# Seven products for twelve instead of eight K tiles in the gate and value projections of an mLSTM layer

## The chip, the cores and the metric

The kernel runs on one core of a Trainium2 chip. The core has TensorE (PE) for matmuls, VectorE (DVE) and ScalarE (ACT) for elementwise work, GpSimd (POOL), SyncE (SP), which here only issues loads, and 16 DMA engines. The metric is device time in microseconds (us): the median of several executions. Lower is better.

## The reference

A trunk of two layers works on x of 256 tokens by 2048 channels, in float32. Each layer has a mixer and a gated feed-forward part. The second layer's mixer is an mLSTM with 8 heads of width 256; its input projection is the part that changes:

```python
def mlstm_mixer(h, w_in, b_gate, h_norm, w_out):
    proj = h @ w_in                       # 256 x 2048 times 2048 x (4*2048 + 32)
    q = heads(proj[..., :MLSTM_W]) * (MLSTM_HEAD_DIM ** -0.5)
    k = heads(proj[..., MLSTM_W:2 * MLSTM_W])
    v = heads(proj[..., 2 * MLSTM_W:3 * MLSTM_W])
    o_gate = jax.nn.sigmoid(proj[..., 3 * MLSTM_W:4 * MLSTM_W])
    gates = proj[..., 4 * MLSTM_W:] + b_gate
    ...                                   # forward and backward scans over the tokens, summed
    hn = rms_norm_per_head(hsum) * h_norm
    return (hn * o_gate) @ w_out
```

## The kernel before

**Matmuls.** Every float32 matrix is split into a high part (rounded by a cast on ACT) and a low part (the rest, by a subtraction on DVE), and a product is the sum of three matmuls: high by high, high by low, low by high. For weights this happens as they arrive. `Stream` (L95) runs through one long list of chunks of 128 x 1024 elements (512 KiB): `load` brings a chunk into one of 7 buffers w through SP's queue, `split` (L125) makes hl of it, in one of 4 buffers, by the cast of L136 and the subtraction of L137. `next` (L158) hands out the next chunk; it keeps loads 6 chunks and splits 2 chunks ahead of PE's place in the program. A chunk of the kind `Made` is loaded from a scratch in DRAM that the kernel has filled before. A chunk of the kind `Chain` gets two additions of half chunks on DVE before its split (L132, L133): the sum left by the chunk before is added to its first half, and its first half to its second.

**Order of the work.** PE's instructions run in the order of the program. The other engines' instructions are put in order by the scheduler of the framework, which simulates the program and takes what is ready, so work of DVE may run well before its place in the program. Small tasks (one head's scores, drains of PSUM, transposes) are generators in a `Weave` (L165): each product advances a clock by `tick`, and a task goes on when its time has come, so a number after `yield` sets where its next matmuls stand among the others. PSUM has two buffers "mm" of two banks and four "ps" of one bank.

**The mLSTM layer** (`mlstm_layer`, L775) runs over four pairs of heads, hp = 0 to 3. For each it makes queries and keys of two heads (tiles mq and mk, `stat_group`, 64 matmuls each, 16 chunks of weights in all) and starts the two tasks `head` (L863), which load a row of gates G, build masks from it (arg), multiply queries and keys (qk), scale (A), transpose (atr) and multiply with the values (av). Then, for hp = 0 to 2, `gates_values` (L989) makes the output gates of this pair (mo) and the values of the next pair (mv), 512 columns each, together. Call this stage the gate/value stage, and the one before it the query/key stage.

**Seven products.** Take two K tiles (128 rows of weights each) as a pair, the two halves of the tokens, and the two blocks of columns (gate, value). Done directly this is 8 products. In the way of Strassen it is 7, with sums of weights and sums of inputs. Three sums of weights come from s0, s1 and r: first m0 = s0 + s1, then r's first half + m0's, then r's second half + r's first. `premix` (L471) makes them ahead of time in DRAM, with DMAs that copy and accumulate: ten DMAs per pair, on the queues of ACT and POOL, each paced by the last matmul issued (L486). The sums of inputs are made by `combine` (L951) from the high and low parts and stand in the tile mcomb.

Before, ML_PAIRS = 4: K tiles 0 to 7 are four such pairs, tiles 8 to 15 are direct. A group runs in this order: direct tiles 8 to 11 into mo; for the four pairs the products p4, p6, p5 and one into mo (8 chunks, all made by premix); direct tiles 12 to 15 into mo; for the four pairs p0 and one into mo; then mv: four products of input sums, and the direct tiles 8 to 15. Two tasks drain PSUM: `first` (L1010) takes p4, p5 and p6 out, `second` (L1029) takes mo and p0 and then starts `gated` (L924), which makes the sigmoid with reciprocals on DVE (L933).

Premix for this layer is started inside the first layer's feed-forward part (L1293) with a gap of 30 us of the Weave's clock: one pair starts every 30 us, and its steps take 5 x 30 us. The feed-forward layers use seven products too, with units A and B (tiles pp); there every second pair is a `Chain` already.

Of the kernel before, what the change touches and what calls it, by code (L numbers as in the profile page):

```python
# [9 lines left out]
F32 = mybir.dt.float32  # L10
# [36 lines left out]
ML_PAIRS = 4  # L47
ML_DIRECT = (list(range(2 * ML_PAIRS, 12)), list(range(12, KT)))

# [45 lines left out]
class Stream:  # L95
# [29 lines left out]
    def split(self, then=None):  # L125
        i = self.n_split
        w, n, width = self.w.pop(i)
        if isinstance(self.srcs[i], Sum):
            self.sum = w
        elif isinstance(self.srcs[i], Chain):  # L130
            half = CH * P // 2
            self.behind(self.nc.vector.tensor_add(w[:, :half], w[:, :half], self.sum[:, :half]), self.lows[0])  # L132
            self.nc.vector.tensor_add(w[:, half:], w[:, half:], w[:, :half])  # L133
# [85 lines left out]
def trunk(ctx: ExitStack, tc: tile.TileContext, gx, xT, xn, call, catt, cml, weights, mixes, out):  # L219
# [257 lines left out]
    def premix(layer, gap, late, n):  # L477

        def one(i, s0, s1, r, made):
            m = scratch.tile([P, 2, CH * P], F32, tag=f"m{layer}{i}", name=f"m{layer}_{i}")  # L480
            h = CH * P // 2
            steps = [(nc.scalar, m[:, 0], s0, {}), (nc.scalar, m[:, 1], r, {}), (g, m[:, 0], s1, add),
                     (g, m[:, 1, :h], m[:, 0, :h], add), (g, m[:, 1, h:], m[:, 1, :h], add)]
            for n, (eng, to, src, kw) in enumerate(steps):
                for p in range(0, P, P // 2):
                    paced(eng.dma_start(to[p : p + P // 2], src[p : p + P // 2], **kw))  # L486
                    yield (0.1, 0.6, 0.6, 0.6, 0.6)[n] * gap
            for j in range(2):
                made[j].ap = m[:, j]
# [285 lines left out]
    def mlstm_layer(norm, nxt):  # L775
        with ExitStack() as es:
# [6 lines left out]
            comb = actp.tile([P, ML_PAIRS, 2, 4, P], F32R, tag="B1", name="mcomb")  # L783
# [79 lines left out]
            def head(h, q, kk, vt, hh):  # L863
# [6 lines left out]
                yield 2.5  # L870
# [80 lines left out]
            def combine(j):  # L951
# [9 lines left out]
                a.copy(comb[:, j, 0], sf)  # L961
                v.tensor_sub(comb[:, j, 1], sf, comb[:, j, 0].bitcast(F32))
# [18 lines left out]
            def direct(ps, kts, first, last):  # L981
                for i, k in enumerate(kts):
                    if i % 2 == 0:
                        hl = st.next()
                    wh, wl = (hl[:, j, i % 2 * 512 : i % 2 * 512 + 512] for j in range(2))
                    for t in range(2):
                        product(ps[:, t], x_part(k, t), wh, wl, first[t] and i == 0, last[t] and i == len(kts) - 1)

            def gates_values(hp):  # L989
# [5 lines left out]
                js = range(ML_PAIRS)  # L995

                mo = mmp.tile([P, 2, 512], F32, tag="mm", name=f"mo{hp}")
                direct(mo, ML_DIRECT[0], (True, True), (False, False))

                p46 = mmp.tile([P, 2, 512], F32, tag="mm", name=f"mp46{hp}")  # L1000
                p5 = psp.tile([P, 512], F32, tag="ps", name=f"mp5{hp}")
                for j in js:
                    xs = [[comb[:, j, i, m] for i in range(2)] for m in (1, 0, 2)] + [x_part(2 * j + 1, 1)]
                    for n, (ps, x_) in enumerate(zip((p46[:, 0], p46[:, 1], p5, mo[:, 1]), xs)):
                        if n % 2 == 0:
                            hl = st.next()
                        wh, wl = (hl[:, i, n % 2 * 512 : n % 2 * 512 + 512] for i in range(2))
                        product(ps, x_, wh, wl, n < 3 and j == 0, n < 3 and j == js[-1])

                def first():  # L1010
                    t5 = t1p.tile([P, 512], F32, tag="t5", name=f"mt5{hp}")
                    a.copy(t5, p5)
                    yield 1.2
                    for to, op, one, two in ((x10, v.tensor_sub, p46[:, 1], t5), (x01, v.tensor_sub, t5, p46[:, 0]),
                                             (x11, v.tensor_sub, x01, p46[:, 1])):
                        tc.keep_in_program_order(op(to, one, two))
                        yield 1.0

                wv.add(first(), 0.3)
                direct(mo, ML_DIRECT[1], (False, False), (False, True))  # L1020

                p0 = psp.tile([P, 512], F32, tag="ps", name=f"mp0{hp}")
                for j in js:
                    hl = st.next()
# [584 lines left out]
```

## Time and profile before

| | |
|---|---|
| median of 3 runs | 2148.92 us (2148.67 to 2149.26) |
| profiled execution | 2149.43 us, span 2147.6 us |
| PE busy | 2140.5 us |
| DVE, ACT, POOL busy | 1802.4, 1445.1, 306.3 us |
| DMA | 612.95 MB, mean 285 GB/s |
| gate/value stages (three) | 1043.07 to 1087.29, 1136.12 to 1180.34, 1229.17 to 1273.40 us |

The profile shows one execution. A row of a timeline gives start, duration, engine, line, operation, the tile written <- the tiles read, the shape and how many such records were merged; brackets hold idle time of the engine before it and what ended that. Rows of groups give busy us and mean ns of one, and after the second bar the idle time before. A row of waits gives total us, times, longest. Line numbers are those of kernel.py; matmuls have one line (L274), so they are told apart by their tiles. PEld is the load of the stationary operand, which runs beside the matmuls.

### The profile page before, as it was taken

How to read it: one execution, taken by the hardware profiler on the slowest of the kernel's cores; microseconds unless marked ns; L12 is line 12 of the kernel's file. 1: busy time of each engine (PE TensorE's matmuls, PEld its weight loads, DVE VectorE, ACT ScalarE, POOL GpSimd, SP SyncE). 2: the span in 40 equal slices, each digit the busy share in tenths (PEclk: the TensorE clock that was granted, in tenths of full speed). 3: DMA queues.
4: the chain of work that ended last, by engine and by line, in shares of the span. 5: the costliest groups of instructions: out<-in, count | busy, mean ns of one | idle time of the engine just before them, and what ended most of it. 6: DMA issues, size and time to landing. Idle time of an engine off the chain costs nothing.

```text
span 2147.6 us, 32448 instructions
## 1 busy us (share of the span) xinstructions
PE 2140.5 (100%) x11364; PEld 1834.2 (85%) x11364; DVE 1802.4 (84%) x2536; ACT 1445.1 (67%) x2199; POOL 306.3 (14%) x390
## 2 busy tenths in 40 slices
PE   9999999999999999999999999999999999999999
PEld 7888888888888888889888888888888888888887
DVE  7786678889988889898888797667888898889988
ACT  6665577777777777766556564557776777777774
POOL 0022112111111122111111011211111111100000
PEclk9999999999999999999999999999999999999999
DMA  9678889899999999998988798988999999888775
GB/s 333 209 213 257 260 250 321 270 326 337 312 331 329 339 350 339 312 301 240 289 244 296 234 310 237 279 244 248 312 288 335 335 314 317 286 256 270 254 250 187
DMA packets 184422, 612.95 MB, mean 285 GB/s; under 512 B 24282, under 2 KB 27138, under 8 KB 184258
## 3 DMA queue, kind: packets, MB, share of 16 engines
q1 hardware_dynamic: 133952, 478.60, 61.9%
q0 software_dynamic: 30304, 73.69, 20.1%
q10 hardware_dynamic: 20002, 58.60, 7.9%
q8 instruction: 89, 1.46, 0.3%
q14 instruction: 75, 0.61, 0.1%
HBM read 608.64 MB, written 111.19 MB: 335 GB/s over the span
## 4 chain that ended last, share of the span: by engine, by line
PE 94%; DVE 2%; DMA 2%; issue 1%; ACT 0%; ACTq 0%; DVEq 0%; SPq 0%
PE up L274 43%; PE pp L274 15%; PE op L274 8%; PE mk L274 4%; PE mq L274 4%; PE mo L274 3%; PE qproj L274 3%; PE dn L274 3%; PE mv L274 3%; PE mp L274 2%; DVE hl L137 1%; PE kproj L274 1%; PE vproj L274 1%; PE pool L274 1%; DMA w<-in_up 1%
## 5 line engine op out<-in xcount | busy, mean ns | idle before, releaser
L137 DVE TENSOR_TENSOR hl<-w,hl 128x1024 fp32r<-128x1024 f32 (+1 forms) x869 | 1045.7, 1214 | 167.4 <-ACT hl L136 158.0
L136 ACT CAST hl<-w 128x1024 fp32r<-128x1024 f32 (+1 forms) x868 | 892.0, 1046 | 391.6 <-PE up L274 112.5
L274 PE MATMUL up<-xx,hl 128*128 128x512 f32 (+1 forms) x5632 | 994.0, 337 | 0.0
L274 PEld LDWEIGHTS up<-xx,hl 128*128 128x128 f32 x5632 | 866.9, 188 | 130.6 <-DVE hl L137 0.7
L486 POOL DMA_DIRECT2D m<-m x208 | 166.4, 816 | 931.2 <-PE up L274 431.8
L274 PE MATMUL pp<-hl,s 128*128 128x512 f32 x912 | 227.2, 390 | 1.3 <-DVE hl L137 1.0
L274 PEld LDWEIGHTS pp<-hl,s 128*128 128x128 f32 x912 | 167.9, 188 | 36.3 <-DVE hl L137 3.7
L274 PE MATMUL pp<-hl,g 128*128 128x512 f32 x684 | 174.0, 390 | 0.0
L274 PEld LDWEIGHTS pp<-hl,g 128*128 128x128 f32 x684 | 125.9, 188 | 24.5
L440 ACT COPY tb_up<-up 128x512 f32<-128x512 f32 x88 | 51.6, 587 | 112.6 <-PE up L274 112.6
L1122 DVE TENSOR_TENSOR y<-y,z 128x510 f32<-128x510 f32 x88 | 60.7, 690 | 62.9 <-ACT y L1121 62.4
L486 POOL DMA_DIRECT2D m<-in_dn x80 | 69.0, 863 | 245.8 <-PE up L274 57.9
L1121 ACT ACTIVATE y<-tb_up,conv 128x256 f32<-128x256 f32 x176 | 103.7, 589 | 0.0
L274 PE MATMUL mk<-xx,hl 128*128 128x512 f32 (+1 forms) x512 | 93.3, 338 | 1.2 <-DVE hl L137 1.2
L274 PE MATMUL mq<-xx,hl 128*128 128x512 f32 (+1 forms) x512 | 92.2, 337 | 0.0
L274 PE MATMUL op<-hl,cat 128*128 128x512 f32 x384 | 91.5, 393 | 0.0
L1119 ACT ACTIVATE z<-tb_up,conv 128x256 f32<-128x256 f32 x176 | 88.4, 502 | 4.0 <-DVE tb_up L1114 2.0
L274 PEld LDWEIGHTS mk<-xx,hl 128*128 128x128 f32 x512 | 79.2, 188 | 12.9 <-DVE hl L137 1.6
L274 PE MATMUL op<-hl,mcat 128*128 128x512 f32 x384 | 89.7, 392 | 0.0
L441 DVE TENSOR_TENSOR tb_up<-up,tb_up 128x512 f32<-128x512 f32 x88 | 60.7, 690 | 34.1 <-ACT tb_up L440 33.7
L274 PEld LDWEIGHTS mq<-xx,hl 128*128 128x128 f32 x512 | 79.3, 188 | 11.6
L1120 ACT ACTIVATE z<-tb_up,conv 128x256 f32<-128x256 f32 x176 | 87.4, 497 | 0.0
(257 smaller groups left out, 2196.3 us busy)
## 6 DMA issues: line engine op xcount, KB each, us to landing
w<-in_up SPq DMA_DIRECT2D x352, 512.0 KB, 6.7
w<-in_dn SPq DMA_DIRECT2D x174, 512.0 KB, 6.4
w<-in_m_in SPq DMA_DIRECT2D x118, 512.0 KB, 5.9
w<-m SPq DMA_DIRECT2D x104, 512.0 KB, 5.8
m<-in_dn ACTq DMA_DIRECT2D x160, 256.0 KB, 5.8
m<-m POOLq DMA_DIRECT2D x208, 128.0 KB, 6.1
w<-in_a_in SPq DMA_DIRECT2D x45, 512.0 KB, 5.2
m<-in_dn POOLq DMA_DIRECT2D x80, 256.0 KB, 7.2
```

What stands on the lines that cost most here:

```text
L136: (self.nc.vector.tensor_copy if i + c == 0 else self.nc.scalar.copy)(hl[:, 0, c : c + n], w[:, c : c + n])
L137: low = self.nc.vector.tensor_sub(hl[:, 1, c : c + n], w[:, c : c + n], hl[:, 0, c : c + n].bitcast(F32))
L274: last_mm[0] = pe.matmul(out_, lhsT, rhs, start=start, stop=stop, skip_group_check=True)
L440: a.copy(tb, ps[:, :, 1, :])
L441: v.tensor_add(tb, ps[:, :, 0, :], tb)
L486: paced(eng.dma_start(to[p : p + P // 2], src[p : p + P // 2], **kw))
L1119: a.activation(z[:, 0, j, :], u[:, j, :], AF.Copy, scale=cw(tl, 0))
L1120: a.activation(z[:, 1, j, :], u[:, j, :], AF.Copy, scale=cw(tl, 2))
L1121: a.activation(y[:, j, :], u[:, j, :], AF.Identity, scale=cw(tl, 1), bias=cw(tl, 3))
L1122: v.tensor_add(y[:, :, 1:S], y[:, :, 1:S], z[:, 0, :, 0 : S - 1])
```

## The change

ML_PAIRS becomes 6, so K tiles 0 to 11 are in seven products and tiles 12 to 15 direct. The order of a group is now written as a string: A is the first part of a pair (four products, two chunks), B the second part (two products, one chunk), P the last sum of two pairs (two products, one chunk), D and E a direct chunk of two K tiles for mo and for mv (four products each). The direct chunks stand between the pairs, and mv is opened by the first E, before the last B. Tiles are opened on first use, and counters tell the first and last product of each.

Of the odd pairs premix makes only the first sum (four DMAs instead of ten); r comes from the input as a `Chain`, so its two sums are made on DVE. mcomb has two parts for six pairs. The split queries hl_q have one buffer instead of two. The wait in `head` before the masks is 6.0 instead of 2.5 for head 0. Premix starts at the same place with a gap of 23 instead of 30, for 18 pairs instead of 12.

```diff
-ML_PAIRS = 4
-ML_DIRECT = (list(range(2 * ML_PAIRS, 12)), list(range(12, KT)))
+ML_PAIRS = 6
+ML_ORDER = [(e[0], int(e[1:] or 0)) for e in "A0 A1 D A2 A3 A4 D A5 B0 B1 B2 B3 B4 E B5 P0 P2 E P4".split()]
+ML_SUMS = {"A": ("p4", "p6", "p5", "m1"), "B": ("p0", "m0"), "P": ("v0", "v0"), "D": ("m0", "m1") * 2, "E": ("v0", "v1") * 2}
...
-        if isinstance(self.srcs[i], Sum):
+        if isinstance(self.srcs[i], (Sum, Made)):
             self.sum = w
...
-            steps = [(nc.scalar, m[:, 0], s0, {}), (nc.scalar, m[:, 1], r, {}), (g, m[:, 0], s1, add),
-                     (g, m[:, 1, :h], m[:, 0, :h], add), (g, m[:, 1, h:], m[:, 1, :h], add)]
+            steps = [(nc.scalar, m[:, 0], s0, {}), (g, m[:, 0], s1, add)]
+            gaps = (0.6, 0.6)
+            if len(made) == 2:
+                steps[1:1] = [(nc.scalar, m[:, 1], r, {})]
+                steps += [(g, m[:, 1, :h], m[:, 0, :h], add), (g, m[:, 1, h:], m[:, 1, :h], add)]
+                gaps = (0.1, 0.6, 0.6, 0.6, 0.6)
...
-            comb = actp.tile([P, ML_PAIRS, 2, 4, P], F32R, tag="B1", name="mcomb")
+            combs = [actp.tile([P, 4, 2, 4, P], F32R, tag="B1", name="mcomb0")]
+            combs.append(kp.tile([P, ML_PAIRS - 4, 2, 4, P], F32R, tag="mcomb", name="mcomb1"))
...
-                r = tp.tile([P, 2, 2, S], F32R, tag=name[0] + "hl", name=f"hl_{name}")
+                r = tp.tile([P, 2, 2, S], F32R, tag=name[0] + "hl", bufs=2 - (name[0] == "q"), name=f"hl_{name}")
...
-                yield 2.5
+                yield 6.0 if h == 0 else 2.5
...
+                for kind, j in ML_ORDER:
+                    if kind == "A":
+                        xs = [[comb(j)[:, i, m] for i in range(2)] for m in (1, 0, 2)] + [x_part(2 * j + 1, 1)]
+                    elif kind == "B":
+                        xs = [x_part(2 * j + k, 0) for k in range(2)]
+                    elif kind == "P":
+                        xs = [[comb(j + k)[:, i, 3] for i in range(2)] for k in range(2)]
+                    else:
+                        xs = [x_part(at[kind] + k, t) for k in range(2) for t in range(2)]
+                        at[kind] += 2
+                    for n, (e, x_) in enumerate(zip(ML_SUMS[kind], xs)):
+                        half = n // 2 if kind in "DE" else n % 2
+                        if n == 0 or (kind == "A" and n == 2):
+                            hl = st.next()
+                        wh, wl = (hl[:, i, half * 512 : half * 512 + 512] for i in range(2))
+                        left[e] -= 1
+                        product(tile_of(e), x_, wh, wl, left[e] + 1 == total[e], left[e] == 0)
+                    if (kind, j) == ("A", ML_PAIRS - 1):
+                        wv.add(first(), 0.3)
+                    elif (kind, j) == ("B", ML_PAIRS - 1):
+                        wv.add(second(), 0.3)
...
-                        premix(2, 30.0, 30.0, 0)
+                        premix(2, 23.0, 23.0, 0)
...
+            made = [Made()] if j % 2 else [Made(), Made()]
+            part = [p[hp * ML_PAIRS + j] for p in parts]
+            mixes.append(part + [made])
+            out += made + [Chain(part[2])] * (j % 2)
```

More of the change, by code (lines that the diff above doesn't have):

```diff
@@ L486, in one @@
                     paced(eng.dma_start(to[p : p + P // 2], src[p : p + P // 2], **kw))
-                    yield (0.1, 0.6, 0.6, 0.6, 0.6)[n] * gap
-            for j in range(2):
-                made[j].ap = m[:, j]
+                    yield gaps[n] * gap
+            for j, e in enumerate(made):
+                e.ap = m[:, j]
         for i, e in enumerate(mixes[layer]):
@@ L979, in x_part @@
                 return [norm.xx[:, k, i, t * P : t * P + P] for i in range(2)]
[L981 to L987, printed above, removed]
             def gates_values(hp):
@@ L994, in gates_values @@
                 wv.until(lambda: "combos" in done)
-                js = range(ML_PAIRS)
-                mo = mmp.tile([P, 2, 512], F32, tag="mm", name=f"mo{hp}")
[L998 to L1008, printed above, removed]
+                left = {}
@@ L1016, in first @@
                         tc.keep_in_program_order(op(to, one, two))
                         yield 1.0
[L1019 to L1024, printed above, removed]
-                    for n, ps in enumerate((p0, mo[:, 0])):
-                        wh, wl = (hl[:, i, n * 512 : n * 512 + 512] for i in range(2))
-                        product(ps, x_part(2 * j + n, 0), wh, wl, n == 0 and j == 0, j == js[-1])
@@ L1346, in _ml_chunks @@
     a, made = [_stat(w_in[:, c + MD : c + 512], range(KT))], [[], [], []]
[L1347 removed]
+    k0 = 2 * ML_PAIRS * P
     for hp in range(MH // 2):
```

55 lines of the change are left out of this document (31 added, 24 removed).

## Prediction

> **What bounds the kernel now.** I read the page first, then the busy times by stage, the waits of TensorE, and last the timelines of TensorE and VectorE in the stages that the edit touches.
>
> ```profile
> span 2147.6 us, 32448 instructions
> PE 2140.5 (100%) x11364; PEld 1834.2 (85%) x11364; DVE 1802.4 (84%) x2536; ACT 1445.1 (67%) x2199; POOL 306.3 (14%) x390
> ```
>
> TensorE (PE) is idle for 2147.6 - 2140.5 = 7.1 us in all. So the time is the sum of its matmuls, and an edit pays by removing some, as long as everything else stays hidden. The table below has the three gate/value stages (first, third, fifth row) and the query/key stages between them.
>
> ```profile
> 1043.07:1087.29 44.22, 44.22 (x209) 37.04 (x209) 40.39 (x63) 29.72 (x38) 6.82 (x10) 1.00 0.97 320
> 1087.29:1136.12 48.83, 48.83 (x293) 43.15 (x293) 39.30 (x62) 25.65 (x35) 6.78 (x10) 1.00 0.76 218
> 1136.12:1180.34 44.22, 44.22 (x209) 37.03 (x209) 39.95 (x63) 29.43 (x38) 4.33 (x6) 1.00 0.92 305
> 1180.34:1229.17 48.83, 48.83 (x294) 43.15 (x293) 39.73 (x62) 25.77 (x35) 4.59 (x6) 1.00 0.78 237
> 1229.17:1273.40 44.23, 44.23 (x210) 37.04 (x209) 40.01 (x63) 29.61 (x38) 5.83 (x8) 1.00 0.96 315
> ```
>
> After the length come the busy times of PE, weight loads, DVE, ACT, POOL, then clock, DMA share and GB/s. PE fills each gate/value stage; VectorE (DVE) is next with 40.39, 39.95 and 40.01 of 44.22 us. The query/key stages leave DVE 9 us. PE's waits, whole run:
>
> ```profile
> PE mk L274 <- DVE hl L137: 1.2, 1, 1.2
> PE pp L274 <- DVE hl L137: 1.0, 1, 1.0
> ```
>
> No wait lies in a gate/value stage; the one on mk is in the first query/key stage.
>
> **The sum: products removed.** One product is three matmuls of 128x512. Per group the old order has 8 + 16 + 8 + 8 + 4 + 16 = 60 (direct, seven-product first part, direct, second part, last sum, direct). The new one has 6 pairs x 7 + 4 tiles x 4 = 58. From the chain:
>
> ```profile
> 1073.69 13.60 PE mv L274 x60
> ```
>
> 60 matmuls in 13.60 us are 0.2267 us each, 0.68 us a product. Three groups save 6 products: **-4.1 us**. A stage would shrink from 44.22 to 42.86 us. This part is certain; the rest asks what of it survives.
>
> **Weight splits and the adds on VectorE.** A group reads 25 chunks instead of 22, so 3 more casts on ACT and 3 more subtractions on DVE. The odd pairs (three per group) also add two 128x512 halves each on DVE.
>
> ```profile
> L137 DVE TENSOR_TENSOR hl<-w,hl 128x1024 fp32r<-128x1024 f32 (+1 forms) x869 | 1045.7, 1214 | 167.4 <-ACT hl L136 158.0
> L132 DVE TENSOR_TENSOR w<-w,sum 128x512 f32<-128x512 f32 x36 | 24.6, 684 | 3.9 <-DMA w<-in_dn 3.9
> L136 ACT CAST hl<-w 128x1024 fp32r<-128x1024 f32 x22 | 23.0, 1054 | 12.4 <-PE mo L274 5.3 <-PE mp L274 2.4 <-PE mv L274 2.0
> ```
>
> The last row is ACT in the second gate/value stage: 12.4 us of waiting before its casts, mostly for PE, so 3 x 1.05 us of casts hide there. On DVE the durations overstate, since the next record starts before the last has ended:
>
> ```profile
> 1078.20 0.68 DVE L1034 TENSOR_TENSOR og<-og,mp 128x512 f32<-128x512 f32 x1
> 1078.80 0.68 DVE L1034 TENSOR_TENSOR mvf<-mvf,mp 128x512 f32<-128x512 f32 x1
> 1079.40 1.22 DVE L137 TENSOR_TENSOR hl<-w,hl 128x1024 fp32r<-128x1024 f32 x1
> 1080.53 0.68 DVE L1034 TENSOR_TENSOR mvf<-mvf,mp 128x512 f32<-128x512 f32 x1
> ```
>
> Start to start a 512-wide add takes 0.60 us and a split 1.13. So a group gains 3 x 1.13 + 6 x 0.60 = 7.0 us of DVE work: 40.1 + 7.0 = 47.1 us against 42.86. That doesn't fit, unless something leaves the stage. Something does:
>
> ```profile
> 1176.59 1.22 DVE L137 TENSOR_TENSOR hl<-w,hl 128x1024 fp32r<-128x1024 f32 x1
> 1177.72 4.97 DVE L933 RECIPROCAL og<-og 128x256 f32<-128x256 f32 x3
> 1182.61 1.16 DVE L137 TENSOR_TENSOR hl<-w,hl 128x1024 fp32r<-128x1024 f32 x1
> ```
>
> These reciprocals begin 2.6 us before the stage ends (1180.34). The task that releases them started 20 products (13.6 us) before the end; now only 10 products (6.8 us) follow it, so they fall into the next stage, where 9 us are free. That takes 2.6 us away: 44.5 against 42.86, short by 1.6 us. Four split buffers let DVE enter the stage three chunks (3.4 us) ahead and leave with less, which covers 1.6 on paper. What remains is crowding: in the first half of the stage chunks last 1.36 us, and the head's masks and score products are queued among the splits. The nearest row for it is the feed-forward part, which has had the same adds 36 times:
>
> ```profile
> 559.47 0.69 DVE L132 TENSOR_TENSOR w<-w,sum 128x512 f32<-128x512 f32 x1
> 560.07 0.68 DVE L1123 TENSOR_TENSOR y<-y,z 128x510 f32<-128x510 f32 x1
> 560.67 1.22 DVE L137 TENSOR_TENSOR hl<-w,hl 128x1024 fp32r<-128x1024 f32 x1
> 561.81 0.68 DVE L133 TENSOR_TENSOR w<-w 128x512 f32<-128x512 f32 x1
> ...
> PEld pp L274 <- DVE hl L137: 3.7, 6, 1.4
> ```
>
> The adds are slipped between other work, and the weight loads waited 3.7 us in 36 uses: for 9 uses 0.9 us, 0.3 a group. That is the low end, because there long chunks stand between the pairs. The high end is all that doesn't fit, 47.1 - 42.86 = 4.2 a group. I take 0.5, near the feed-forward row: **+1.5 us**. Such an add also waits for its own load (3.9 us in 4 of 36 in the row of L132); behind it on DVE stand the next splits, and behind those PE.
>
> **A PSUM wait.** mv is now opened after the fifth second-part pair, while mo is still open, so it needs the buffer of p4 and p6, which the three operations of first() must have read.
>
> ```profile
> 1152.61 0.61 PE L274 MATMUL mp<-hl,mcomb 128*128 128x512 f32 x2
> 1159.68 1.60 PE L274 MATMUL av<-mvt,at 128*128 128x256 f32 x12
> 1160.80 0.67 DVE L1016 TENSOR_TENSOR mvf<-mvf,mp 128x512 f32<-128x512 f32 x1
> ```
>
> The last p product ends near 1153.2 and the buffer is read out at 1161.47, 8.3 us later. The new cover is ten products, 6.8 us, plus 1.44 if the head's av lands there. So the wait is 0 to 1.5 us a group. Since these reads sit only behind splits, I take 0.2: **+0.6 us**. Behind that wait PE has the rest of the group queued.
>
> **The first head.** Its yield grows from 2.5 to 6.0, which puts its qk matmuls 3.5 us later in PE's order; nothing is added. The one wait of PE in this part comes from here:
>
> ```profile
> 1009.64 0.35 DVE L873 SCALAR_TENSOR_TENSOR arg<-G,mc,kml 128x128 f32<-128x128 f32 x1 [0.88 <-DMA G<-gd]
> 1011.14 1.15 DVE L873 SCALAR_TENSOR_TENSOR arg<-G,mc,kml 128x256 f32<-128x256 f32 x3 [1.15 <-DMA G<-gd]
> ```
>
> DVE stands 2.0 us for a load and the splits queue behind it, which gives PE's 1.2 us. These operations already run well before their place in the program, so a later place need not move them: between -1.2 and 0. Two more combines land in that neighbourhood:
>
> ```profile
> L962 DVE TENSOR_TENSOR mcomb<-msf,mcomb 128x512 fp32r<-128x512 f32 x4 | 2.7, 683 | 0.0
> L955 DVE TENSOR_TENSOR mf<-xx 128x512 f32<-128x512 f32 x4 | 2.7, 663 | 0.0
> L958 DVE TENSOR_TENSOR msf<-mf 128x256 f32<-128x256 f32 x4 | 1.6, 412 | 0.0
> L960 DVE TENSOR_TENSOR msf<-mf,msf 128x128 f32<-128x128 f32 x4 | 1.1, 286 | 0.0
> ```
>
> With L959, the same shape as the last row, one combine is 2.3 us of DVE; should one be queued ahead of the late splits it adds up to that, 0 to +2.3. I set both edits together at **0**. The single query buffer costs nothing: the next pair is written after its 64 matmuls, and the qk that frees the buffer stands before their end, except for head 0, whose successor's qk stands only in the gate stage.
>
> **DMA.** Premixing now has 18 jobs 23 us apart instead of 12 jobs 30 apart. Even jobs take 5 x 23 = 115 us instead of 150, odd ones have only their first sum. The last even job starts at 17 x 23 and ends at 506 on that clock, before: 360 + 150 = 510. Payload is 3 MiB per 46 against 2 MiB per 30, the same rate. ACT's queue gets 54 issues for 48, POOL's 72 as before:
>
> ```profile
> L486 ACTq DMA_DIRECT2D m<-in_m_s x48: 497/498/577, 677.9 to 1065.5; - x48
> ```
>
> Six times 0.5 us spread over some 400 us hide in ACT's waits above; bound 0 to 3 us if each delayed a needed cast, taken as 0. SP issues 9 more loads, and no row shows anything waiting for SP's issue. The rate is nearer to a limit. 22 chunks of 512 KiB are 11.5 MB or 261 GB/s, so 44 to 59 GB/s of the stages' 305 to 320 is other traffic. Afterwards 13.1 MB + 1.9 to 2.6 MB in 42.86 us is 350 to 367 GB/s. The busiest 20 us elsewhere, PE full in each:
>
> ```profile
> 520.00:540.00 20.00, 20.00 (x108) 17.15 (x107) 16.50 (x23) 16.23 (x28) 2.33 (x3) 1.00 1.04 365
> 1520.00:1540.00 20.00, 20.00 (x109) 17.20 (x108) 17.56 (x25) 14.00 (x22) 2.32 (x3) 1.00 1.02 367
> 640.00:660.00 20.00, 20.00 (x111) 17.27 (x110) 18.04 (x25) 13.91 (x21) 2.36 (x3) 1.00 1.05 335
> ```
>
> The need equals the best rows, and seven load buffers start the stage full, so I take 0; the bad end is a rival. The Trainium skill, "DMA: Bandwidth & Descriptors", Specifications, gives about 358 GB/s as the HBM limit of a core; two of these rows lie above it, so the measurement decides. By that limit the upper need, 15.7 MB, would take 43.9 us, 1.0 us a group more.
>
> **Total.** -4.1 + 1.5 + 0.6 = -2.0 us. The profiled execution took 2149.43 us (its span and 1.8 around it), 0.5 above the median; it would become 2147.4, and the median **2146.9 us**.
>
> **Rivals.** Within 0.2%, 4.3 us, this kernel can't be told from no change.
>
> *All of it hidden.* DVE's lead covers every add, p4 and p6 are read in time, and the load of G no longer stops the splits: -4.1 - 1.2 = -5.3, 2143.6 us. For it: a feed-forward part that lives with the same adds and DVE shares as high. Against: there the adds have long chunks between them. It counts as faster from -4.3 on, so it needs the G wait gone as well.
>
> *VectorE becomes the bound (other side).* If the reciprocals are not pushed out and the lead is used up, each group stalls 4.2 us in the seven-product part: 3 x 4.2 - 4.1 = +8.5, 2157.4 us. It decides above (4.1 + 4.3) / 3 = 2.8 us a group. Against: reciprocals have no one waiting at once, and splits are needed first.
>
> *DMA becomes the bound.* At the 335 GB/s of the third row 15.4 MB take 46.0 us, 3.1 over: 9.4 - 4.1 = +5.3, 2154.2 us. Against: no PE idle in any of those rows, and a query/key stage at 218 to 237 GB/s on either side refills the buffers.
>
> **How the numbers follow.** Forecast or near it (within 0.2%): 0.50. All hidden: 0.27. VectorE bound: 0.15. DMA bound: 0.08. So faster 0.27, same 0.50, slower 0.23. The likeliest case alone runs from 2144.8 (no stall, the G wait stays) to 2150.5 (1.9 us a group). The range goes from 2143.5, just past all hidden, to 2153.5, short of the two slower ends, which leaves out about 2 in 10.
>
> **What would show it.** Right: gate/value stages of 43 to 44 us; PE waits on hl of 1 to 3 us in all; DVE at 97% or more there; reciprocals after the stage's end. Wrong if those stages stay at 44.2 or longer with DVE at 100% (VectorE), if splits or adds wait for loads of w (DMA), if PE waits for L1016 at the first mv matmul beyond 1.5 us, or if the wait in the first query/key stage changes by more than 1.2.

## The result and the profile after

The changed kernel takes **2182.36 us** (median of 5, 2180.68 to 2186.62), the kernel before in the same session 2149.26 us (2148.67 to 2153.99). The ratio is 1.0153, with a 95% interval of 1.0142 to 1.0165: 33 us slower. Forecast were 2146.9 us and a range of 2143.5 to 2153.5. The profiled execution took 2180.68 us, with a span of 2178.9 against 2147.6, so its own excess is 31.3 us. From the page of after:

```profile
span 2178.9 us, 32511 instructions
PE 2145.6 (98%) x11346; PEld 1832.4 (84%) x11346; DVE 1825.0 (84%) x2573; ACT 1453.8 (67%) x2210; POOL 308.7 (14%) x390
```

PE's idle time has grown from 7.1 to 33.3 us, and its busy time by 5.1 us although it has 18 matmuls fewer, partly because some of them ran at a lower clock (below). To see where the time goes, I compare the starts of landmarks. The first product of mv, which opens the mLSTM layer, stands at 982.4 us, before at 966.9: **15.5 us are lost ahead of the layer**, in the first feed-forward part, which the diff touches only through premix. The first output product of the layer (op from mcat) stands at 1377.0, before at 1345.8, so **15.7 us more are lost inside the layer**. After it nothing is lost.

*The feed-forward part.* Busy times by stretch (length, then PE, weight loads, DVE, ACT, POOL, the granted clock, DMA share and GB/s), first before, then after:

```profile
700.00:740.00 40.00, 40.00 (x219) 34.25 (x218) 33.36 (x44) 26.70 (x40) 7.95 (x10) 1.00 1.04 341
```

```profile
700.00:740.00 40.00, 31.93 (x161) 26.05 (x160) 26.07 (x34) 20.76 (x32) 8.00 (x10) 0.90 1.00 309
...
732.00:734.00 2.00, 0.00 (x0) 0.00 (x0) 0.00 (x0) 0.00 (x0) 0.00 (x0) 0.50 1.01 328
...
740.00:742.00 2.00, 2.00 (x8) 1.80 (x7) 2.00 (x4) 2.00 (x5) 0.00 (x0) 0.50 0.75 293
742.00:744.00 2.00, 2.00 (x13) 1.74 (x13) 2.00 (x3) 1.33 (x2) 0.00 (x0) 1.00 0.89 320
```

PE stood idle for 8.1 of these 40 us. From 732 to 734 no engine did anything, and the DMA engines were full (share 1.01). The clock fell to 0.50 and stayed there until 742: while it was low PE issued 8 matmuls in 2 us, afterwards 13. So the wait of 6.7 us below was followed by a slow restart, which cost about half of the 5.1 us that it lasted (an estimate). The Trainium skill, "TensorE: Matmul & The Clock Gate", Part 1, says that TensorE falls to half its clock after an idle window of about 3.4 us and needs about as long of work to come back; the half clock agrees, and here 5.1 us passed between the first matmul (736.91) and the first stretch at 1.00 (742). Why PE waited shows the timeline of ACT, with ACT's DMA issues as ACTq, and that of PE:

```profile
726.41 1.05 ACT L137 CAST hl<-w 128x1024 fp32r<-128x1024 f32 x1 [2.78 <-DMA w<-in_dn]
731.22 0.50 ACTq L491 DMA_DIRECT2D m<-in_dn  x1
734.79 0.50 ACTq L491 DMA_DIRECT2D m<-in_m_s  x1
735.33 0.58 ACT L441 COPY tb_up<-up 128x512 f32<-128x512 f32 x1 [7.87 <-DMA m<-in_dn]
735.81 2.94 ACT L137 CAST hl<-w 128x1024 fp32r<-128x1024 f32 x3
```

```profile
736.91 1.22 PE L275 MATMUL up<-xx,hl 128*128 128x512 f32 x2 [6.71 <-ACT hl L137]
```

Two of premix's own issues stood in ACT's queue ahead of the casts that PE needed. The first waited until 731.22, and the chain of waits says for what (who released whom is inferred by the profile):

```profile
712.25 18.89 DMA w<-in_up
731.14 0.02 issue
731.16 0.02 ACTq L491
731.18 0.04 issue
731.22 6.04 DMA m<-in_dn
```

A load of weights took 18.89 us from issue to landing. It isn't alone: the four loads from in_up issued between 712.25 and 717.46 took 18.9 to 22.2 us, while in the kernel before none in this feed-forward part (560 to 970 us) took longer than 13.2. Further waits of PE for splits, 4.1 us, lie between 800 and 860.

*The mLSTM layer.* The stages of after, three gate/value stages and then the query/key stages ahead of each:

```profile
1061.92:1108.10 46.18, 43.34 (x204) 35.78 (x203) 40.49 (x67) 30.29 (x41) 6.49 (x8) 1.00 0.93 299
1158.17:1206.35 48.18, 43.97 (x205) 35.61 (x203) 41.41 (x66) 31.68 (x41) 6.36 (x7) 1.00 0.91 309
1255.67:1303.10 47.43, 44.08 (x204) 35.62 (x203) 41.03 (x66) 31.62 (x41) 7.12 (x8) 1.00 0.94 301
1007.73:1061.92 54.19, 50.86 (x295) 44.52 (x293) 43.56 (x85) 27.70 (x36) 7.61 (x10) 0.97 0.83 248
1108.10:1158.17 50.07, 49.36 (x294) 43.11 (x292) 45.50 (x69) 27.85 (x39) 6.13 (x8) 1.00 0.89 268
1206.35:1255.67 49.32, 49.09 (x294) 43.20 (x292) 44.48 (x68) 25.96 (x36) 4.04 (x6) 1.00 0.77 253
```

The gate/value stages were to shrink from 44.22 to 43 or 44 us; they last 46.2, 48.2 and 47.4. But VectorE isn't the full engine there: 40.5 to 41.4 us of 46 to 48. It waits itself. Three rows of the waits of PE (whole run; the rows of up and pp belong to the feed-forward parts and are left out), and one row of those of DVE (980 to 1380 us):

```profile
PE atr L912 <- DVE A L904: 10.1, 4, 3.0
PE mp L275 <- DVE hl L138: 2.9, 2, 1.9
PE htr L952 <- DVE hn L947: 1.2, 1, 1.2
```

```profile
DVE w L133 <- DMA w<-in_m_s: 9.9, 5, 3.8
```

L133 is the first of the two additions of an odd pair, in_m_s is where r is loaded from. The second stage in the timeline, with the rows of DVE and PE in order of time:

```profile
1174.98 0.69 DVE L133 TENSOR_TENSOR w<-w,w 128x512 f32<-128x512 f32 x1 [3.24 <-DMA w<-in_m_s]
...
1175.66 1.22 DVE L138 TENSOR_TENSOR hl<-w,hl 128x1024 fp32r<-128x1024 f32 x1
...
1176.93 0.73 PE L275 MATMUL mp<-hl,mcomb 128*128 128x512 f32 x2 [1.90 <-DVE hl L138]
...
1182.61 0.34 DVE L904 SCALAR_TENSOR_TENSOR A<-arg,denr,A 128x128 f32<-128x128 f32 x1
1182.87 0.34 DVE L906 SCALAR_TENSOR_TENSOR A<-arg,denr,A 128x128 f32<-128x128 f32 x1
1183.00 0.66 PE L912 MATMUL atr<-cst,A 128*128 128x128 f32 x4 [2.15 <-DVE A L904]
```

VectorE stands 3.24 us at an addition whose load hasn't landed. The split behind it comes late and stops mp for 1.90 us. The scales of the head's scores (A), behind more splits, come late too and stop the transposes atr for 2.15. Of the 9.9 us at such additions 3.8 lie in the first query/key stage, 0.3, 3.5 and 2.3 in the three gate/value stages.

So there are two questions: what in premix costs 15.5 us, and what in the group costs 15.7.

### The profile page after: what moved, and what is told of

Its sections match the earlier page's. It is cut to its first block, busy times and chain, and to the rows that moved or that the text cites. A ratio compares the mean times of both kernels' runs of the same rounds, so it can differ in the third digit from the quotient of the medians.

```text
span 2178.9 us, 32511 instructions
## 1 busy us (share of the span) xinstructions
PE 2145.6 (98%) x11346; PEld 1832.4 (84%) x11346; DVE 1825.0 (84%) x2573; ACT 1453.8 (67%) x2210; POOL 308.7 (14%) x390
## 4 chain that ended last, share of the span: by engine, by line
PE 85%; DVE 6%; DMA 5%; issue 2%; ACT 1%; ACTq 0%; POOL 0%; DVEq 0%; POOLq 0%; SPq 0%
PE up L275 42%; PE pp L275 14%; PE op L275 8%; PE qproj L275 3%; DVE hl L138 3%; PE dn L275 3%; PE mk L275 3%; PE mq L275 2%; PE mo L275 2%; PE mv L275 2%; DMA w<-in_up 1%; DMA w<-in_m_s 1%; PE kproj L275 1%; PE vproj L275 1%; PE mp L275 1%
## 5 line engine op out<-in xcount | busy, mean ns | idle before, releaser
L491 POOL DMA_DIRECT2D m<-m x196 | 159.8, 836 | 945.4 <-PE up L275 385.5
```

## The experiments

For each run I give the ratio to the kernel before, whose medians were 2148.8 to 2149.4 us in these comparisons. From the profiles I use the excess ahead of the layer (start of mv minus 966.9) and the length of the layer from the first mv to the first op product, 378.9 us before and 394.6 after.

### The pace of premix alone (b_gap23)

The kernel before with the new gap:

```diff
-                        premix(2, 30.0, 30.0, 0)
+                        premix(2, 23.0, 23.0, 0)
```

> The kernel before, with its 12 premix jobs 23 us apart instead of 30, at the same starting place; nothing else. Theory A (the pace): the quicker jobs fill the DMA engines in the feed-forward part, ACT's queue stands behind its own DMA issue, and the splits of the weights with it. Then some 13 us are lost between 645 and 965 us, about 2162 us in all, with an idle time of PE of several us before up that ACT's cast ends. Rival (the pace is harmless, the loss comes from what the odd jobs do or from the longer list of 18 jobs): 2147 to 2151 us.

Measured: 2171.98 us, ratio 1.0098 (1.0083 to 1.0113). mv starts at 987.8, 20.9 us late. PE's longest waits between 700 and 960:

```profile
PE pp L274 <- ACT hl L136: 4.9, 4, 2.9
PE pp L274 <- DVE hl L137: 4.3, 6, 0.8
PE up L274 <- DVE hl L137: 2.7, 4, 0.9
```

One number, with nothing else of the change, makes the loss in the feed-forward part, and a larger one than in the changed kernel, whose jobs are lighter (14 DMAs a pair of jobs instead of 20).

### The old gap, started earlier (a_gap30)

The changed kernel with a gap of 30, which needs a start nine up tiles earlier to be done in time:

```diff
-                    if layer == 0 and (c, i) == (len(FCH) - 3, 6):
-                        premix(2, 23.0, 23.0, 0)
+                    if layer == 0 and (c, i) == (len(FCH) - 4, 5):
+                        premix(2, 30.0, 30.0, 0)
```

> The changed kernel with 18 premix jobs 30 us apart instead of 23, started nine feed-forward tiles earlier so that the last is done in time. Theory A: the idle time of 8 us in the feed-forward part goes, and 10 to 15 us of the 33 come back, 2167 to 2172 us. Rival (any premix of this layer beside the feed-forward layer's own premix overloads the DMA): no better than 2180 us, as the two now run side by side for longer.

Measured: 2179.53 us, ratio 1.0132 (1.0115 to 1.0149). mv starts at 987.6, 20.7 us late, with the waits spread from 601 to 766 us. A slow pace doesn't help where the transfers run beside those of the feed-forward part's own premix (m from in_dn), whose last issues stand at 758 before and 768 after.

### The new gap, started later (b_late23)

The kernel before with a gap of 23, started three up tiles later, about 47 us:

```diff
-                    if layer == 0 and (c, i) == (len(FCH) - 3, 6):
-                        premix(2, 30.0, 30.0, 0)
+                    if layer == 0 and (c, i) == (len(FCH) - 2, 1):
+                        premix(2, 23.0, 23.0, 0)
```

> The kernel before with premix's gap of 23 (which alone gave 2172.0, 20.9 us of it lost in the first feed-forward part), but started three tiles of the up projection later, about 47 us. Theory O (what hurts is the overlap with the transfers that make the first feed-forward part's own sums, which end near 770 us): two jobs less fall into the overlap, the loss halves at least, 2150 to 2161. Rival P (the pace hurts wherever it runs): 2167 to 2173, the loss shifted by some 50 us.

Measured: 2154.91 us, ratio 1.0022 (1.0013 to 1.0032). mv starts at 970.9: of 20.9 us, 4.0 are left. So the pace as such isn't the cause; what counts is where premix runs, and the overlap with the feed-forward part's own premix is the reading that fits. No run moved that other premix, so this is argued from the place alone. The issues of premix for the mLSTM layer between 640 and 735 us (count, durations, first and last start), with the gap of 23 at the old place and then at the later one:

```profile
L486 ACTq DMA_DIRECT2D m<-in_m_s x10: 497/497/498, 670.9 to 733.0; - x10
L486 POOL DMA_DIRECT2D m<-in_m_s x2: 778/1408/2039, 708.3 to 721.7; - x2
```

```profile
L486 ACTq DMA_DIRECT2D m<-in_m_s x3: 498/498/498, 717.9 to 723.8; - x3
```

Twelve transfers before 735 us go with a loss of 20.9 us, three with 4.0. Between 735 and 860 the later start has 29, the earlier one 27. The count alone isn't the measure: the kernel before has eight before 735 and loses nothing, and the later start's waits lie behind 740, 2.5 us of them between 800 and 860. What goes with the loss is late loads: of the loads from in_up issued between 700 and 740 us the median to landing is 17.5 us with the gap of 23 at the old place, 9.6 at the later one, 10.4 in the kernel before.

### Both in the changed kernel (a_late20)

The changed kernel, three tiles later and with a gap of 20, so that the last jobs end in time:

```diff
-                    if layer == 0 and (c, i) == (len(FCH) - 3, 6):
-                        premix(2, 23.0, 23.0, 0)
+                    if layer == 0 and (c, i) == (len(FCH) - 2, 1):
+                        premix(2, 20.0, 20.0, 0)
```

> The changed kernel with premix started three tiles of the up projection later (about 47 us, as in the run of before that lost only 4 us that way) and a gap of 20, so that the last jobs still end in time. Theory O (overlap with the first feed-forward part's own sums): the loss there falls from 15.5 us to under 5, the first mv product before 972, 2170 to 2174. Rival P (the pace): a shorter gap makes it worse, 2181 to 2190.

Measured: 2163.47 us, ratio 1.0067 (1.0052 to 1.0082), better than expected. mv starts at 968.5: the loss ahead of the layer has gone from 15.5 to 1.6 us, at a faster pace. The layer keeps its loss (393.7 us long). No load from in_up between 560 and 970 us takes longer than 13.8 us.

### The queue of premix's copies (a_pool)

The changed kernel, copies on POOL's queue instead of ACT's (for the second feed-forward part's premix, too):

```diff
-            steps = [(nc.scalar, m[:, 0], s0, {}), (g, m[:, 0], s1, add)]
+            cp = nc.scalar if layer == 0 else g
+            steps = [(cp, m[:, 0], s0, {}), (g, m[:, 0], s1, add)]
...
-                steps[1:1] = [(nc.scalar, m[:, 1], r, {})]
+                steps[1:1] = [(cp, m[:, 1], r, {})]
```

> The changed kernel, with premix's copies for the second feed-forward part and for the mLSTM layer issued on POOL's queue in place of ACT's; nothing else moves. Theory Q (ACT's casts stand behind an issue in its own queue that waits 8 us): the 15.5 us lost between 720 and 860 us shrink to under 5, so 2169 to 2173. Rival D (the DMA engines are full there, and ACT's queue is only where it shows): the loss stays, 2179 to 2185, with the waits on loads of w instead of on m.

Measured: 2170.43 us, ratio 1.0099 (1.0084 to 1.0115). mv starts at 977.2: the loss there is 10.3 us instead of 15.5, so each theory has a part. Between 700 and 740 us, and PE's waits from 690 to 970:

```profile
700.00:740.00 40.00, 36.25 (x190) 29.47 (x188) 28.02 (x36) 22.35 (x35) 10.16 (x14) 1.00 1.03 317
```

```profile
PE up L275 <- DVE hl L138: 3.6, 5, 0.9
PE pp L275 <- DVE hl L138: 3.3, 5, 1.0
PE up L275 <- ACT hl L137: 1.5, 1, 1.5
```

The long wait of 6.7 us is gone, and with it the drop of the clock (1.00 instead of 0.90 in the first row). What remains are many waits of about 1 us for late splits, with the DMA share at 1.03; loads from in_up still take up to 22.3 us. The profiled execution is 8.8 us shorter than that of the changed kernel, 5.2 of it there and 3.6 in the layer (391.0 us).

### The additions alone (b_chain)

The kernel before, still four pairs in the old order and a gap of 30, with the odd pairs' second and third sums on VectorE (so premix has fewer DMAs, too):

```diff
-            made = [Made(), Made()]
-            mixes.append([p[hp * ML_PAIRS + j] for p in parts] + [made])
-            out += made
+            made = [Made()] if j % 2 else [Made(), Made()]
+            part = [p[hp * ML_PAIRS + j] for p in parts]
+            mixes.append(part + [made])
+            out += made + [Chain(part[2])] * (j % 2)
```

> The kernel before with its order and its four pairs, where the two odd pairs of a group get their last two sums on VectorE; premix has correspondingly less to do. Theory B (VectorE is crowded in the first part of the pairs): 2.4 us of adds come into each gate/value stage and PE waits 1 to 2 us a group for A or a split, 2152 to 2155 us. Rival (the adds alone fit, as in the feed-forward part; only six pairs in a row with three chains are too much): 2147 to 2150 us.

Measured: 2149.02 us, ratio 0.9997 (0.9988 to 1.0007). Twelve additions cost nothing in the gate/value stages, which are 44.2 us as before, with DVE at 41.2, 41.0 and 40.7, and no row of VectorE waiting for a load of r exists. The layer is 3.1 us longer (382.0), all of it in the first query/key stage, where VectorE waits 4.7 instead of 2.0 us for loads of G; mv starts 1.4 us earlier.

### Without the additions, and without their wait (a_noadds, a_dummy)

Two runs that compute something else. The first leaves the additions of the mLSTM layer out. The second keeps them, in the same places and sizes, but lets them work on the chunk before alone, so that they don't need r:

```diff
-            out += made + [Chain(part[2])] * (j % 2)
+            out += made + [part[2]] * (j % 2)
```

> The changed kernel without the two additions that make the odd pairs' second and third sums of weights (the chunks are split as they come; 18 additions of 0.6 us less on VectorE in the mLSTM layer, output changed, all transfers as they were). Theory V (VectorE has no room for them): the 10.1 us of TensorE's waits for A, and the 2.9 for hl under mp, fall below 3, the mLSTM layer's loss of 15.7 us to under 5: 2166 to 2172. Rival W (the order of the group puts the transposes too near to A and the splits first, adds or not): the waits for A stay above 7, 2178 to 2183.

```diff
+        elif isinstance(self.srcs[i], Dummy):
+            half = CH * P // 2
+            self.behind(self.nc.vector.tensor_add(self.sum[:, :half], self.sum[:, :half], self.sum[:, half:]), self.lows[0])
+            self.nc.vector.tensor_add(self.sum[:, half:], self.sum[:, half:], self.sum[:, :half])
...
-            out += made + [Chain(part[2])] * (j % 2)
+            out += made + [Dummy(part[2])] * (j % 2)
```

> The changed kernel in which the two additions per odd pair stand at the same places with the same sizes, but work on the chunk before alone and no longer wait for the load of r (output changed; all transfers as they were). Theory V (VectorE's time, 3.6 us a group): gate/value stages stay at 46 to 48 us, 2179 to 2184. Rival L (it is the wait for the load of r, 0.3, 3.5 and 2.3 us in the three stages, with the splits queued behind it): stages of 43 to 44 us as without the additions, 2164 to 2170.

Measured: 2164.63 us without them, ratio 1.0074 (1.0055 to 1.0093), and 2169.15 with dummies, ratio 1.0096 (1.0079 to 1.0113); the layer lasts 380.8 and 380.6 us, so **either edit takes 14 us from it**. The gate/value stages, first without the additions, then with dummies:

```profile
1063.26:1106.35 43.09, 43.09 (x205) 35.85 (x204) 36.68 (x61) 30.23 (x41) 6.19 (x8) 1.00 1.00 330
1157.23:1200.25 43.02, 43.02 (x205) 35.92 (x204) 39.01 (x62) 31.65 (x41) 5.50 (x7) 1.00 0.97 342
1249.08:1292.46 43.38, 43.28 (x205) 35.85 (x203) 38.75 (x62) 31.70 (x41) 6.99 (x8) 1.00 1.00 328
```

```profile
1059.67:1102.90 43.23, 43.23 (x204) 35.85 (x203) 39.53 (x66) 30.42 (x42) 6.19 (x8) 1.00 0.95 324
1153.14:1196.33 43.19, 43.19 (x205) 35.84 (x203) 41.68 (x68) 31.69 (x41) 6.33 (x7) 1.00 0.96 330
1245.28:1290.47 45.19, 43.68 (x205) 35.68 (x203) 41.78 (x68) 31.91 (x41) 6.04 (x8) 1.00 0.98 324
```

The second kernel gives VectorE as much to do as the changed one (41.68 against 41.41 us in the second stage), and the stage takes 43.19 us instead of 48.18. The third stage takes 45.19, above the forecast: PE waits there 1.4 us at the first product of mv for a small operation of VectorE (re_h). So it isn't VectorE's time. It is what the additions depend on and what depends on them: dummies needn't wait for r's load, and the cast of r's chunk needn't wait for them. The next run looks at the first alone. The medians of the two runs differ by 4.5 us, but their layers by 0.2, so I read the layers.

### A later place for the additions (a_pin)

The changed kernel; only the order on VectorE differs: the first addition may stand no earlier than behind the subtraction of the chunk just before it, where the original allows it from four chunks before.

```diff
-            self.behind(self.nc.vector.tensor_add(w[:, :half], w[:, :half], self.sum[:, :half]), self.lows[0])
+            self.behind(self.nc.vector.tensor_add(w[:, :half], w[:, :half], self.sum[:, :half]),
+                        self.lows[-1 if isinstance(self.srcs[i], Late) else 0])
...
-            out += made + [Chain(part[2])] * (j % 2)
+            out += made + [Late(part[2])] * (j % 2)
```

> The changed kernel in which the first addition of an mLSTM chain is held, in VectorE's order, behind the subtraction of the chunk just before it in place of that of four chunks before. Same work, same transfers. Theory L (the additions are put into VectorE's queue before their load has landed, and all behind them waits): the 9.9 us that VectorE waits for loads of r in the mLSTM layer fall below 4, gate/value stages of 43 to 45 us, 2167 to 2173. Rival S (an addition put later makes its own split late): TensorE waits for hl under mp instead, stages of 46 to 48, 2179 to 2185.

Measured: 2172.36 us, ratio 1.0103 (1.0089 to 1.0117). VectorE no longer waits for loads of r, and PE no longer for A. The layer lasts 385.5 us, 9.1 less. Its gate/value stages are 45.1, 45.2 and 45.6 us: some 2 us each above those without additions, which is rival S: late splits, in the second stage as waits of the weight loads:

```profile
PEld mp L282 <- DVE hl L145: 2.2, 4, 1.0
```

So of the 13.8 us that go with the additions 9.1 come back when VectorE no longer stands at r's load. The other 4.7 (385.5 against 380.8) stay; no run tells whether they are the price of the later place or of the chain of additions, cast and subtraction wherever it stands.

### The heads (a_atr14, a_h25)

Two edits of the places of a head's work in PE's order: the odd heads' transposes four units later, and head 0's masks where they were before the change.

```diff
-                yield 10.0 if h % 2 else 6.0
+                yield 14.0 if h % 2 else 6.0
```

> The changed kernel with the transposes of A of odd heads 4 us later in PE's order (yield 14 instead of 10). Theory B says that VectorE is late by 2.0 to 2.9 us with A in each gate/value stage because splits and adds stand before it: if only the place is wrong, the three waits of PE for A go and 6 to 8 us come back, 2174 to 2176 us. If VectorE has no room at all, the wait only moves to a split or to av: 2180 us or more.

```diff
-                yield 6.0 if h == 0 else 2.5
+                yield 2.5
```

> The changed kernel with head 0's wait before the masks back at 2.5. If its place made TensorE's 2.96 us wait for A at 1056.6, that wait goes and head 0's first stage has a clock of 1.00 again: 2178 to 2179.5. Rival (DVE is behind with splits there, whatever the place): 2181 to 2184. As first forecast, up to 2.5 us more by the load of G.

Measured: 2176.77 us for the first, ratio 1.012 (1.0105 to 1.0135). The three waits of odd heads for A vanish and head 0's falls to 1.6, 8.5 us in all, and the layer gets 6.9 us shorter (387.7); the rest comes back as waits for hn (2.1), at (1.8) and mvf (1.1). For the second 2181.47 us, ratio 1.015 (1.0135 to 1.0165). The waits for A fall from 10.1 to 4.3 us, yet the layer is only 1.0 us shorter (393.7): waits turn up at qk (1.1), cols (small transposes at the start of the layer; 2.2, after 0.4) and mo (0.7). Moving the operation that waits helps only where there is slack behind it.

### The additions on POOL (a_gadds)

```diff
+            eng = self.nc.gpsimd if isinstance(self.srcs[i], PoolChain) else self.nc.vector
+            first = eng.tensor_add(w[:, :half], w[:, :half], self.sum[:, :half])
...
-            out += made + [Chain(part[2])] * (j % 2)
+            out += made + [PoolChain(part[2])] * (j % 2)
```

> The changed kernel with the additions of the odd pairs of the mLSTM layer on POOL in place of VectorE. Theory V: VectorE gets its 3.6 us a group back, gate/value stages of 43 to 44.5 us, 2165 to 2172. Rival G (POOL's queue stands in premix's issues, which wait for matmuls, or an addition takes far longer there): casts and splits of the odd pairs come late, stages of 47 to 55 us in the first two groups, 2180 to 2205.

Measured: 2178.99 us, ratio 1.0137 (1.012 to 1.0154), the layer 394.9 us: between the two forecasts. The additions, and VectorE's splits beside them (groups between 1040 and 1320 us; busy, mean ns, idle before):

```profile
L140 POOL TENSOR_TENSOR w<-w,w 128x512 f32<-128x512 f32 x9 | 15.1, 1683 | 58.0 <-DMA w<-in_m_s 35.7 <-DMA w<-in_m_in 9.3 <-DVE A L912 6.7
L146 DVE TENSOR_TENSOR hl<-w,hl 128x1024 fp32r<-128x1024 f32 x119 | 146.9, 1247 | 14.1 <-ACT hl L145 13.8
```

The first addition takes 1.68 us there, on VectorE 0.68. Now it is POOL that waits for r (35.7 us), which rival G didn't name, and the splits come late all the same: PE waits 3.8 us for hl under mp.

### Both cures together (a_fix, a_fix2)

The later start with a gap of 20 and the later place of the additions; then, on top, htr later:

```diff
                     tc.keep_in_program_order(v.tensor_mul(hn, hn, o))
-                    yield 6.0
+                    yield 9.0
```

> Both cures together: premix three tiles later with a gap of 20, and the additions held behind the chunk before. If the two losses are separate, the first cure's 2163.5 falls by the 9 to 13 us of the second: 2150 to 2155. If they share a cause (transfers that are late), less than 5 us come on top: 2158 to 2163.

> As the run with both cures, and the transposes of a gated head (htr) 3 us later, since the reciprocals now stand in the query/key stage and htr waits for hn: 1 to 3 us less than that run, 2148 to 2154; a rival is that the wait moves to the next operation, and the time stays within 1 us of that run.

Measured: 2164.16 us, ratio 1.0066 (1.0053 to 1.0078), and with htr later 2160.42, ratio 1.0052 (1.0038 to 1.0066). The first is above either forecast and no faster than the later start alone (2163.47): the layer lasts 392.3 us instead of the 385.5 of the second cure alone. The loss has moved into the first group, whose query/key stage takes 54.6 us and whose gate/value stage 49.4; the other two stages are 45.2 and 45.8. There PE waits 4.0 us at the first product of mv for a cast; in the second run it waits 3.9 us at the same product, by the profile for another thing:

```profile
1082.89 4.47 PE L282 MATMUL mv<-hl,xx 128*128 128x512 f32 x12 [3.86 <-DVE mvf L1030]
```

So the two losses aren't independent. What ties them isn't shown; in the layer's first group, query/key and gate/value stage together, 31 issues of premix stand with the later start and 25 without it (a_pin), and the load that the cast waited for took 11.16 us. The gain of htr is real: three query/key stages of 48.8 us instead of 48.8, 48.8 and 50.2, and a shorter first one. No version here beats the kernel before.

## Where the prediction was right and where wrong

In the profiled executions the excess is 31.3 us: +15.5 ahead of the layer, +13.8 in the layer by the additions (394.6 against 380.8 without them), +1.9 for the rest of the layer (380.8 against 378.9, with the saved products in it). The forecast for the whole was -2.0. Two terms of its sum failed, premix at 0 and the additions at +1.5. Point by point:

- **Products removed, -4.1, called certain: right but for about a fifth.** Without the additions the gate/value stages are 43.09, 43.02 and 43.38 us instead of 44.22, together 3.2 less; the forecast was 42.86 each. What ends there is given back in the query/key stages: the four of them take 52.4, 50.9, 48.8 and 50.2 us against 50.6, 48.8, 48.8 and 48.8 before, together +5.1.
- **Premix at 0: the step that failed first, 15.5 us.** I wrote that six more issues "hide in ACT's waits", and that 3 MiB per 46 us are "the same rate" as 2 MiB per 30. Mean rates were the wrong view. What counted was what ran beside the transfers at its start: the DMA share there was 1.04 before the change already (the prediction itself shows 1.05 for 640 to 660), and I looked for DMA as a bound in the gate/value stages only. With twelve transfers of this premix before 735 us (9 on ACT's and 3 on POOL's queue) in place of eight (7 and 1) the loss was there, though the count alone doesn't measure it (b_late23). I also priced an issue on ACT at its 0.5 us; what it cost was the time that it waits in the queue, 7.87 us once, with casts behind it and the clock at 0.50 afterwards. The bound of 3 us on these issues was five times too low for the whole. b_gap23 shows the cause alone, b_late23 and a_late20 show that it lies in where premix runs, a_pool that about a third goes with ACT's queue. That the overlap with the feed-forward part's own premix makes the loads late fits all these runs, but 4.1 of the 15.5 us lie behind 800 us, where that premix has ended.
- **Splits and additions, +1.5 (0.3 to 4.2 a group): the mechanism was named, the size was not seen.** "Such an add also waits for its own load" stands there, with the splits behind it and PE behind those. I took the feed-forward part's waits of weight loads as its size, 3.7 us in 36 uses, and gave the additions' own waits for loads, 3.9 us in those 36 uses, no price. Here these were 9.9 us in 9 uses, and the additions cost 13.8 us of time, 9.1 of which come back without this wait (a_pin). What decides is whether r has landed where the scheduler put the addition. In b_chain it had, in the changed group it hadn't: its loads of r took 7.6 us (median, 1040 to 1310 us) against 5.0 in b_chain. The DMA share doesn't tell the two apart (0.91 to 0.94 against 0.89 to 0.96), so why they took longer is open.
- **VectorE as the bound (rival, 0.15): the right side, by the wrong mechanism.** Its 4.2 us a group resemble the measured 4.6, but the dummy additions take the same time of VectorE and cost almost nothing. "DVE at 97% or more" was wrong: it was at 86 to 88%.
- **The reciprocals: right in place, wrong at 0.** They left the stage, which ended at 1108.10, as the row of DVE at 1114.28 below shows. But hn (a head's output times its gate), and so its transposes htr, wait for them: 1.2 us in PE's waits, and 3.7 us between the medians of the last two runs (a_fix, a_fix2), which differ only in htr's place. "Reciprocals have no one waiting at once" didn't hold in the new place.
- **The PSUM wait of mv, +0.6:** absent in after, and in the run without additions; with dummies PE waits 1.4 us at the same product, by the profile for re_h. It shows in five other runs, 0.4 to 1.3 us in all, and in the last one with 3.9 us at once, beyond the bound of 1.5.
- **Head 0 and the single query buffer, 0:** right in sum. Undoing the head's part moved the median by 0.9 us; no wait for the query buffer appears. Its parts came out otherwise: VectorE's wait for G is gone, but in the first query/key stage PE waits 2.96 us for A and the stage takes 54.2 instead of 50.6 us, a sign that the prediction named. With dummies it takes 50.9, so this goes with the additions.
- **The DMA rival (0.08):** its stages ran at 299 to 309 GB/s, not at the limit that it named, and PE didn't wait for transfers directly. But the sign that the prediction gave for it, additions that wait for loads of w, came true: late loads were the cause all the same, through VectorE's queue here and ACT's in the feed-forward part. By the 358 GB/s of the Trainium skill, "DMA: Bandwidth & Descriptors", Specifications, there was room in every one of these stages. The trace has the engines full below it: a share of 1.00 at 309 GB/s between 700 and 740 us, and at 328 in a gate/value stage without additions.

The reciprocals of the first group in the timeline of after:

```profile
1114.28 4.97 DVE L943 RECIPROCAL og<-og 128x256 f32<-128x256 f32 x3
```

Why the share is full at 309 GB/s in one stretch and at 341 in another, and what made loads take 18.9 to 22.2 us, isn't settled: copies and accumulations between places in DRAM are in both, and no run took them apart.

## What to carry to other kernels

Price an issue or an operation that depends on a transfer by what stands behind it in its queue when the transfer is late, not by its own duration, and place it after the time at which its load has landed in the trace, but not much later: with the later place 4.7 us of the loss stayed here. Judge background transfers by what runs beside them at each moment: here the DMA share was already 1.04, and starting the same kind of transfers 47 us later took the loss from 20.9 to 4.0 us in the kernel before and, at a slightly faster pace, from 15.5 to 1.6 in the changed one. An engine that is 86% busy can still be what others wait for.

## What was not expected of the hardware

- One idle time of PE of 6.7 us was followed by some 5 us at a granted clock of 0.50, though the DMA engines and, from 735 us on, ACT were working.
- With the DMA share at 1.0, four 512 KiB loads in a row took 18.9 to 22.2 us, where the median of the same part's loads from in_up (560 to 970 us) is 8.2 us.
- The same 128x512 addition takes 1.68 us on POOL and 0.68 on VectorE. The Trainium skill, "GPSIMD Engine Reference", Engine selection, gives about a factor of two for such operations; here it is 2.5.
